# Writes of the down projections' operands issued from ACT's queue instead of SP's

## The chip, the cores and the metric

The kernel runs on one core of one Trainium2 chip. Its engines work side by side, each through its own list of instructions in order: PE (matrix products), DVE (vector work), ACT (activations, casts and copies), POOL and SP. SP computes nothing; here it issues the transfers (DMAs) between DRAM and the core's memory SBUF. An issue on any engine starts a transfer, which lands some microseconds later; instructions that need it wait on a semaphore. The metric is the device time of one execution in microseconds, given as the median of several runs.

## The reference, cut to what matters

A trunk of two layers on one sequence of 1024 positions with 1024 channels, all in float32. Layer 0 mixes positions by a Fourier transform and neighbourhood attention, layer 1 by a gated short convolution. Each layer then has a cross-attention to 256 memory tokens and a gated feed-forward block with a convolution over positions. The change touches the operands of the last product of the short-convolution mixer and of both feed-forward blocks:

```
def short_gated_conv_mixer(h, w_in, conv_w, w_out):
    z = h @ w_in
    gate_b, gate_c, u = ...            # three pieces of 1024 columns
    return (gate_b * dwconv3_centred(gate_c * u, conv_w)) @ w_out

def conv_ffn(h, w_up, conv_w, conv_b, w_down):
    z = h @ w_up                       # 1024 -> 4096
    u = z[..., :D_FF]                  # D_FF = 2048
    g = dwconv3_centred(z[..., D_FF:], conv_w) + conv_b
    return (jax.nn.gelu(g, approximate=False) * u) @ w_down
```

## The kernel before

**Arithmetic.** Every float32 operand is split in two parts that PE takes at its faster rate: ACT casts the high part (line 225) and DVE subtracts it from the value to get the low part (line 226). A product is then three matmuls: high by high (line 230), high by low (line 231), low by high (line 232).

**Seven products for eight.** The large products are done in Strassen's manner: the weight matrix and the data are cut in 2 x 2 blocks, and seven products of sums of blocks replace eight of blocks. The sums of weight blocks are made by POOL's transfers with accumulation into DRAM tensors named ws_u (up) and ws_d (down), and loaded by line 1083. The sums of the data's blocks are made on DVE.

**The feed-forward block.** For each block of 128 channels the up product runs its seven products; `up_post` makes gate, convolution (lines 1008 to 1011: ACT begins it, DVE adds the two neighbours) and gelu (line 1321), multiplies, and leaves two buffers of 128 x 1024. `put_rest` makes from them the sums that the down product needs: t1 (line 1240), t2 (1241), t3 (1243), t4 (1245). Each of the seven pieces, 128 x 512 or 256 KB, goes through `put`. `put` writes it to a DRAM tile xd_d (feed-forward) or xd_oc (mixer), 132 times in all; a few pieces of the last block stay in SBUF by a copy on ACT (`stays`). The down product reads the tiles back at line 1429, 512 KB at a time, and splits them again.

**Buffers.** SBUF has 52 places of 128 x 1024 and a few half ones, used over and over. A buffer that a write reads cannot be overwritten before that write has landed; the next user, often the cast of line 225, waits for it.

**Order.** The program is emitted by generators that run ahead of one another. Then the framework orders each engine's instructions by a simulated timeline of its own (line 1761: `tile.TileContext(nc, schedule_with_timeline_sim=True)`). So an edit in one place can shift the order on other engines too. In this kernel all of the transfers started by the hardware path are issued by SP, in SP's order: loads of weights (line 1083), writes of `put` (line 1226), reads back (line 1429), and spills and reloads of the residual. ACT issues none. Every transfer takes one of eight shared completion semaphores in turn, and an issue waits until the transfer that used the same one before has landed.

Of the kernel before, what the change touches and what calls it, by code (L numbers as in the profile page):

```python
# [43 lines left out]
U = 512  # L44
# [49 lines left out]
class Pool:  # L94
# [29 lines left out]
    def put(self, u, n=1):  # L124
        Pool.tick += 1
        for i in range(u, u + n):
            assert self.used[i]
            self.used[i] = False
            self.freed[i] = Pool.tick


class Kern:
# [1085 lines left out]
    def put(self, tag, s, k, p, src):  # L1218

        o = (k % 2) * U  # L1220
        if self.stays(tag, s, k // 2, p):
            if k % 2 == 0:
                self.xs[tag, p] = yield from self.alloc(F32)
            self.nc.scalar.copy(self.xs[tag, p].f(o, o + U), src)
        else:
            self.nc.sync.dma_start(self.xd_tile(tag, s, p, k // 2)[:, o:o + U], src)
        self.did.add((tag, "x", s, p, k))

    @staticmethod
# [536 lines left out]
```

## Time and profile before

| what | us |
|---|---|
| median of 3 runs | 2195.08 (2186.97 to 2198.77) |
| the profiled execution's own time | 2190.69 |
| its span in the profile | 2188.9 |
| PE busy | 2155.6 (98%) |
| DVE busy | 1461.0 (67%) |
| ACT busy | 966.0 (44%) |
| POOL busy | 342.1 (16%) |

The time of an engine at work is summed over its instructions; issuing transfers and waiting on semaphores is not counted as busy. PE is at work nearly all the time, so what matters is where it is not, and where its granted clock is below 1.00: there the same matmul takes longer and counts as busy. The feed-forward up products lie at about 740 to 1065 us (layer 0) and 1770 to 1990 us (layer 1), the mixer's down product of layer 1 at about 1360 to 1430 us.

### The profile page before, as it was taken

The page shows a single profiled execution, that of the slowest core. Times are in us where ns is not written, and L with a number is a line of the kernel's source. Part 1 is how long each engine was busy: PE and PEld are TensorE (multiplying, and loading weights), DVE is VectorE, ACT ScalarE, POOL GpSimd, SP SyncE. Part 2 cuts the span into 40 slices and gives each one's busy share as a digit, 9 for nine tenths or more (in the row PEclk, how much of TensorE's full clock was granted, in tenths as well). Part 3 has the DMA queues.
Part 4 walks back from the last instruction along what each step waited for, and adds up shares of the span by engine and source line. Part 5 has one row for each costly group of instructions (what it writes and reads, how often), then busy time and mean ns, then how long its engine had stood idle before and what let it go on. Part 6 is the DMA issues. An engine that isn't in the chain of part 4 may idle for free.

```text
span 2188.9 us, 27021 instructions
## 1 busy us (share of the span) xinstructions
PE 2155.6 (98%) x10174; PEld 1783.6 (81%) x10174; DVE 1461.0 (67%) x2001; ACT 966.0 (44%) x1506; POOL 342.1 (16%) x446
## 2 busy tenths in 40 slices
PE   9999999999999999999999999999999999999998
PEld 9988888888888777887888888778888878888887
DVE  6755456575667576667777667777566758757774
ACT  6532444354545333345445223535444534334643
POOL 5222122222211122111111100010111000000003
PEclk9999999999999999999999999999999999999999
DMA  9467677788877677899986567965656635447742
GB/s 376 151 158 186 157 183 221 189 207 234 216 202 221 180 191 219 245 277 355 270 267 151 162 193 204 342 162 150 177 163 184 183 101 182 150 135 258 242 154 77
DMA packets 176163, 441.92 MB, mean 202 GB/s; under 512 B 19616, under 2 KB 87456, under 8 KB 173856
## 3 DMA queue, kind: packets, MB, share of 16 engines
q1 hardware_dynamic: 99616, 305.95, 39.5%
q0 software_dynamic: 76416, 134.25, 29.9%
q8 instruction: 79, 1.29, 0.2%
q14 instruction: 52, 0.43, 0.1%
HBM read 384.54 MB, written 189.79 MB: 262 GB/s over the span
## 4 chain that ended last, share of the span: by engine, by line
PE 89%; DVE 5%; DMA 4%; ACT 1%; issue 1%; SPq 0%; DVEq 0%; ACTq 0%
PE PS L231 29%; PE PS L232 29%; PE PS L230 29%; DVE p L226 2%; PE PS L935 1%; DMA p<-in_w_out_dram 1%; ACT p L225 1%; DMA xd_d<-p 1%; DMA p<-in_w_down_dram 1%; DVE p L1009 1%; DMA p<-xd_d 1%; DVE p L1011 0%; DMA p<-ws_u 0%; DMA p<-xd_oc 0%; PE PS L333 0%
## 5 line engine op out<-in xcount | busy, mean ns | idle before, releaser
L230 PE MATMUL PS<-p,p 128*128 128x512 f32 (+1 forms) x3264 | 1222.7, 379 | 14.3 <-ACT p L225 13.4
L231 PE MATMUL PS<-p,p 128*128 128x512 f32 (+1 forms) x3264 | 1230.1, 378 | 5.1 <-DVE p L226 4.9
L232 PE MATMUL PS<-p,p 128*128 128x512 f32 (+1 forms) x3264 | 1218.5, 377 | 2.3 <-DVE p L226 2.3
L226 DVE TENSOR_TENSOR p<-p,p 128x1024 fp32r<-128x1024 f32 (+1 forms) x549 | 607.9, 1124 | 266.6 <-ACT p L225 219.1
L225 ACT CAST p<-p 128x1024 fp32r<-128x1024 f32 (+1 forms) x566 | 530.5, 959 | 542.3 <-PE PS L232 87.1
L230 PEld LDWEIGHTS PS<-p,p 128*128 128x128 f32 x3264 | 615.5, 189 | 140.0 <-ACT p L225 18.3
L231 PEld LDWEIGHTS PS<-p,p 128*128 128x128 f32 x3264 | 615.5, 189 | 125.7 <-DVE p L226 7.5
L232 PEld LDWEIGHTS PS<-p,p 128*128 128x128 f32 x3264 | 615.1, 189 | 121.4 <-DVE p L226 3.2
L317 ACT ACTIVATE p<-p 128x512 f32<-128x512 f32 (+1 forms) x128 | 74.4, 589 | 102.9 <-DVE p L816 39.9
L323 DVE TENSOR_TENSOR p<-p,p 128x512 f32<-128x512 f32 (+1 forms) x111 | 80.0, 723 | 31.5 <-ACT p L317 29.1
L226 DVE TENSOR_TENSOR p<-PS,p 128x512 fp32r<-128x512 f32 (+3 forms) x92 | 67.8, 744 | 41.4 <-ACT p L225 41.0
L1604 POOL TENSOR_TENSOR p<-p,p 128x512 f32<-128x512 f32 (+1 forms) x15 | 16.4, 1124 | 442.6 <-DVE p L497 425.0
L225 ACT CAST p<-PS 128x512 fp32r<-128x512 f32 (+3 forms) x92 | 57.5, 632 | 56.3 <-PE PS L232 31.4
L1075 POOL DMA_DIRECT2D ws_u<-gates x64 | 43.5, 778 | 205.0 <-ACT gates L1074 204.8
L816 DVE TENSOR_TENSOR p<-PS,p 128x512 f32<-128x512 f32 x64 | 43.5, 685 | 35.6 <-PE PS L232 35.5
L1008 ACT ACTIVATE p<-p,vec 128x1024 f32<-128x1024 f32 x32 | 39.7, 1241 | 61.1 <-DVE p L1317 48.4
L1009 DVE SCALAR_TENSOR_TENSOR p<-p,vec,p 128x1023 f32<-128x1023 f32 x40 | 51.2, 1279 | 21.7 <-ACT p L1008 21.1
L1076 POOL DMA_DIRECT2D ws_u<-in_w_up_dram x64 | 36.5, 591 | 175.2 <-DMA ws_u<-gates 175.1
L1077 POOL DMA_DIRECT2D ws_u<-ws_u x32 | 33.3, 1042 | 182.4 <-DMA ws_u<-in_w_up_dram 111.9
L1077 POOL DMA_DIRECT2D ws_u<-in_w_up_dram x32 | 33.6, 1050 | 140.1 <-DMA ws_u<-in_w_up_dram 113.1
L1321 ACT ACTIVATE p<-p 128x1024 f32<-128x1024 f32 x32 | 33.9, 1060 | 47.9 <-DVE p L1011 47.9
L1074 ACT COPY gates<-p 128x1 f32<-128x1 f32 x136 | 24.8, 191 | 68.4 <-DVE p L816 30.0
(171 smaller groups left out, 1300.8 us busy)
## 6 DMA issues: line engine op xcount, KB each, us to landing
ws_u<-in_w_up_dram POOLq DMA_DIRECT2D x96, 512.0 KB, 5.9
p<-ws_u SPq DMA_DIRECT2D x64, 512.0 KB, 4.4
xd_d<-p SPq DMA_DIRECT2D x104, 256.0 KB, 5.7
p<-xd_d SPq DMA_DIRECT2D x52, 512.0 KB, 6.3
ws_d<-in_w_down_dram POOLq DMA_DIRECT2D x48, 512.0 KB, 5.9
p<-in_w_up_dram SPq DMA_DIRECT2D x48, 512.0 KB, 4.8
ws_u<-ws_u POOLq DMA_DIRECT2D x32, 512.0 KB, 6.8
p<-in_wq_dram SPq DMA_DIRECT2D x32, 512.0 KB, 4.7
```

Of the source, the lines that this page charges most:

```text
L225: self.nc.scalar.copy(hi, src)
L226: (eng or self.nc.vector).tensor_tensor(lo, src, hi.bitcast(F32), op=ALU.subtract)
L230: mm(ps, whi, xhi, start=first, stop=False, skip_group_check=True)
L231: mm(ps, whi, xlo, start=False, stop=False, skip_group_check=True)
L232: mm(ps, wlo, xhi, start=False, stop=last, skip_group_check=True)
L317: nc.scalar.activation(t.f(0, w), src, AF.Square)
L323: nc.vector.tensor_tensor(st[ch].f(0, w), st[ch].f(0, w), t.f(0, w), op=ALU.add)
L816: self.nc.vector.tensor_tensor(hc, ps, hc, op=ALU.add)
L1008: nc.scalar.activation(tmp.f(), src, AF.Identity, scale=v[:, w[1]:w[1] + 1], bias=v[:, bias:bias + 1])
L1009: nc.vector.scalar_tensor_tensor(tmp.f(1, S), src[:, 0:S - 1], v[:, w[0]:w[0] + 1], tmp.f(1, S), op0=ALU.mult, op1=ALU.add)
L1075: g.dma_start(d[0:1, 0:1], gate[0:1])
L1077: g.dma_start(d, more, accum_op=ALU.add, max_dma_last_dim=1024)
```

## The change

`put` issues the same write on ACT in place of SP:

```
@@ -1223,7 +1223,7 @@
                 self.xs[tag, p] = yield from self.alloc(F32)
             self.nc.scalar.copy(self.xs[tag, p].f(o, o + U), src)
         else:
-            self.nc.sync.dma_start(self.xd_tile(tag, s, p, k // 2)[:, o:o + U], src)
+            self.nc.scalar.dma_start(self.xd_tile(tag, s, p, k // 2)[:, o:o + U], src)
         self.did.add((tag, "x", s, p, k))
```

In all 132 issues leave SP's list and stand in ACT's; no instruction is added. The framework's order of the other instructions shifts with it.

On ACT, at layer 0's first finished block of the up product (about 747 to 757 us): p_ is a buffer with its place's number, xd_d_0_6 is the down product's operand 6 of the first half.

```order
 L1321 ACTIVATE p_14_6510<-p_14_6510 128x1024
+L1226 DMA xd_d_0_5_0_6564<-p_19_6552 128x512
 L1074 COPY gates<-p_47_6108 128x1
+L1226 DMA xd_d_0_2_0_6516<-p_37_6031 128x512
+L1226 DMA xd_d_0_3_0_6566<-p_37_6031 128x512
 L1268 COPY p_14_6611<-p_48_6126 128x512
 L225 CAST p_33_6682<-p_25_6572 128x1024
+L1226 DMA xd_d_0_6_0_6556<-p_19_6552 128x512
+L1226 DMA xd_d_0_7_0_6559<-p_27_6553 128x512
+L1226 DMA xd_d_0_4_0_6562<-p_27_6553 128x512
 L1074 COPY gates<-p_43_6592 128x1
 L225 CAST p_37_6650<-p_6_6522 128x1024
```

Six of the block's writes now stand between ACT's gelu, copies and casts; three of them come behind the cast into p_33. The last row is the cast into p_37, the place that two of the writes read.

On SP, the same stretch: loads of weights and the writes that were between them.

```order
 L1083 DMA p_25_6572<-ws_u_1_3_1349 128x1024
 L1083 DMA p_10_6686<-in_w_up_dram 128x1024
-L1226 DMA xd_d_0_5_0_6564<-p_19_6552 128x512
-L1226 DMA xd_d_0_2_0_6516<-p_37_6031 128x512
-L1226 DMA xd_d_0_3_0_6566<-p_37_6031 128x512
-L1226 DMA xd_d_0_6_0_6556<-p_19_6552 128x512
-L1226 DMA xd_d_0_7_0_6559<-p_27_6553 128x512
 L1083 DMA p_1_6618<-ws_u_2_7_1350 128x1024
-L1226 DMA xd_d_0_4_0_6562<-p_27_6553 128x512
 L1083 DMA p_6_6732<-ws_u_2_3_1353 128x1024
```

Five writes stood in one run behind two loads, with the write of place p_19 (operand 6) fourth among them; now loads follow loads.

On DVE, in layer 0's up product at about 810 to 816 us: lines 1009 and 1011 are the convolution's two additions, line 226 the low part of an operand.

```order
 L1009 SCALAR_TENSOR_TENSOR p_17_6906<-p_44_6797,vec,p_17_6906 128x1023
+L1011 SCALAR_TENSOR_TENSOR p_17_6906<-p_44_6797,vec,p_17_6906 128x1023
 L1317 TENSOR_TENSOR p_50_6816<-PS,p_50_6816 128x512
+L226 TENSOR_TENSOR p_27_6992<-p_30_6859,p_19_6991 128x1024
+L226 TENSOR_TENSOR p_44_6986<-p_47_6823,p_14_6985 128x1024
 L1325 TENSOR_TENSOR p_7_6228<-PS,p_7_6228 128x512
-L1011 SCALAR_TENSOR_TENSOR p_17_6906<-p_44_6797,vec,p_17_6906 128x1023
-L226 TENSOR_TENSOR p_27_6992<-p_30_6859,p_19_6991 128x1024
+L1322 TENSOR_TENSOR p_7_6228<-p_7_6228,p_17_6906 128x512
 L1009 SCALAR_TENSOR_TENSOR p_10_6927<-p_50_6816,vec,p_10_6927 128x1023
 L1325 TENSOR_TENSOR p_45_6246<-PS,p_45_6246 128x512
-L226 TENSOR_TENSOR p_44_6986<-p_47_6823,p_14_6985 128x1024
```

The subtraction into p_44 moved up, ahead of two lines 1325 and the line 1009 of p_10.

On PE, at the first place: matmuls that take the operands p_37 and p_19.

```order
 L230 MATMUL PS<-p_11_6404,p_37_6650 128x512
 L231 MATMUL PS<-p_21_6405,p_37_6650 128x512
-L230 MATMUL PS<-p_11_6404,p_37_6650 128x512
-L231 MATMUL PS<-p_21_6405,p_37_6650 128x512
 L230 MATMUL PS<-p_3_6362,p_19_6614 128x512
 L231 MATMUL PS<-p_38_6363,p_19_6614 128x512
```

PE now comes to p_19 after two matmuls with p_37 instead of four.

## Rows read from the trace of the kernel before

**Rows 1.** The page: busy time of each engine; share of DMA queues; the chain's engines.

```profile
PE 2155.6 (98%) x10174; PEld 1783.6 (81%) x10174; DVE 1461.0 (67%) x2001; ACT 966.0 (44%) x1506; POOL 342.1 (16%) x446
...
q1 hardware_dynamic: 99616, 305.95, 39.5%
...
PE 89%; DVE 5%; DMA 4%; ACT 1%; issue 1%; SPq 0%; DVEq 0%; ACTq 0%
```

**Rows 2.** PE's waits, whole run: us in total, times, longest us.

```profile
PE PS L230 <- ACT p L225: 13.4, 9, 4.0
PE PS L231 <- DVE p L226: 4.9, 3, 2.6
```

**Rows 3.** Windows: length, busy us (x instructions) by engine, PEclk, DMA share, GB/s.

```profile
745.00:750.00 5.00, 5.00 (x23) 4.05 (x22) 4.96 (x8) 2.35 (x4) 0.51 (x1) 1.00 0.94 246
750.00:755.00 5.00, 4.43 (x19) 3.11 (x17) 4.31 (x7) 1.39 (x3) 0.09 (x1) 1.00 0.83 286
755.00:760.00 5.00, 1.59 (x4) 1.30 (x5) 1.39 (x2) 2.69 (x3) 1.33 (x2) 0.76 1.05 348
760.00:765.00 5.00, 5.00 (x15) 3.88 (x14) 2.45 (x2) 1.30 (x2) 0.50 (x1) 0.56 0.94 255
810.00:815.00 5.00, 3.44 (x15) 2.51 (x14) 5.00 (x7) 0.80 (x1) 0.57 (x2) 1.00 0.77 264
820.00:825.00 5.00, 3.15 (x15) 2.25 (x14) 2.80 (x4) 1.24 (x2) 0.31 (x1) 1.00 1.02 372
1420.00:1425.00 5.00, 3.54 (x15) 2.52 (x14) 5.00 (x7) 2.10 (x3) 0.00 (x0) 1.00 1.04 209
1425.00:1430.00 5.00, 3.87 (x10) 3.04 (x11) 5.00 (x6) 0.71 (x2) 0.00 (x0) 0.66 0.46 131
1785.00:1790.00 5.00, 3.26 (x13) 2.17 (x12) 3.15 (x5) 0.99 (x2) 0.00 (x0) 1.00 1.03 371
1790.00:1795.00 5.00, 4.64 (x14) 3.61 (x15) 3.58 (x3) 3.23 (x4) 0.00 (x0) 0.68 0.72 235
```

**Rows 4.** The chain of waits: start us, length us, what.

```profile
748.83 0.61 DVE p L1326
...
749.97 7.26 DMA xd_d<-p
757.31 1.05 ACT p L225
...
812.58 1.13 DVE p L226
...
816.18 5.98 DMA p<-ws_u
...
1783.62 5.54 DMA xd_d<-p
```

**Rows 5.** Line 1226's issues (ns min/median/max, first to last us), and their landings.

```profile
L1226 SPq DMA_DIRECT2D xd_d<-p x104: 319/376/1703, 744.6 to 2035.4; - x104
L1226 SPq DMA_DIRECT2D xd_oc<-p x28: 319/320/1342, 1235.6 to 1397.0; - x28
...
DMA to landing us min/median/max: 2.0/5.7/11.2
```

**Rows 6.** Timeline of SP: start us, us, line, operation, how many in a row.

```profile
748.60 0.33 SPq L1083 DMA_DIRECT2D p<-in_w_up_dram  x1
749.02 3.64 SPq L1226 DMA_DIRECT2D xd_d<-p  x5
```

**Rows 7.** DMA issues, 748.5 to 748.9 us, then whole run: KB each, us to landing.

```profile
p<-in_w_up_dram SPq DMA_DIRECT2D x1, 512.0 KB, 6.7
...
p<-ws_u SPq DMA_DIRECT2D x64, 512.0 KB, 4.4
```

**Rows 8.** Timeline of ACT: start us, us, instruction, [idle before it, for what].

```profile
747.04 1.06 ACT L1321 ACTIVATE p<-p 128x1024 f32<-128x1024 f32 x1 [1.12 <-DVE p L1011]
751.50 1.05 ACT L225 CAST p<-p 128x1024 fp32r<-128x1024 f32 x1 [1.36 <-DMA p<-ws_u]
...
970.88 1.05 ACT L225 CAST p<-p 128x1024 fp32r<-128x1024 f32 x1 [5.63 <-DMA xd_d<-p]
```

More of the change, by code (lines that the diff above doesn't have):

```diff
@@ L1225, in put @@
         else:
-            self.nc.sync.dma_start(self.xd_tile(tag, s, p, k // 2)[:, o:o + U], src)
+            self.nc.scalar.dma_start(self.xd_tile(tag, s, p, k // 2)[:, o:o + U], src)
         self.did.add((tag, "x", s, p, k))
```

## The prediction

> **What bounds the kernel now.** I read the page's busy shares first, then PE's waits over the whole run, then a table of 5 us windows, and last the chain of waits and the timelines of SP and ACT around the worst windows. The shares give the ceiling: PE is busy for 2155.6 us, 98% of the span, and the chain that ends last runs through PE for 89% of its length, through DVE for 5%, through DMA for 4% and through ACT for 1% [rows 1]. A queue that carries 39.5% of the DMA engines' time [rows 1] is not the bound of the whole; the change can only move the places where PE stands still or runs slowly.
>
> PE's waits are few. The reader is to see in them that the longest single one is 4.0 us and that the waits for ACT's casts (line 225, the high half of an operand) add to 13.4 us in nine waits, and those of one kind of matmul for DVE's subtraction (line 226, the low half) to 4.9 us in three [rows 2]. The windows turn this into a loss, idle time and slow clock together. A full window of 5 us has 23 matmuls at granted clock 1.00, so one is 5/23 = 0.217 us. Counting what is missing from 23 in each window [rows 3]:
> - A, layer 0's first finished block (750 to 765): 4 + 19 + 8 = 31 matmuls, 6.7 us. The clock falls to 0.76 and 0.56, the lower of the two levels (1.2 GHz for most of the last window), after PE had stood still.
> - F, the same place of layer 1 (1785 to 1795): 10 + 9 = 19, or 4.1 us, clock down to 0.68.
> - D, the mixer's down product (1420 to 1430): 8 + 13 = 21, or 4.6 us, clock down to 0.66.
> - B (810 to 815, 820 to 825): 8 + 8 = 16, or 3.5 us, clock 1.00 throughout.
>
> Together 87 matmuls, 18.9 us, under 1% of the time. No edit of a queue can win more than about that in these stretches.
>
> What ends the waits is read in the chain. At A, ACT's cast waits until a write xd_d, issued at 749.97, has landed 7.26 us later, because the cast overwrites the buffer that the write reads; the cast takes 1.05 us and PE goes on [rows 4]. At F it is the same kind of write, 5.54 us [rows 4]. At B the first gap waits for DVE's subtraction, and the second for a load p<-ws_u that takes 5.98 us [rows 4]. So the writes delay PE at A and F; at B something else does.
>
> **The change part by part.** It takes 132 issues (104 xd_d, 28 xd_oc) off SP and puts them on ACT; it adds no instruction.
>
> *Issue time.* At the median of the 104, 132 x 0.376 = 50 us [rows 5] of ACT's order are now issues. ACT is busy for 966.0 us of 2188.9 [rows 1], so this lies in its idle time: 0 us. If that cover is gone, as in front of a cast that PE waits for, four issues in a row (as at A) cost 4 x 0.32 = 1.3 us once; bounds 0 and +3 us.
>
> *Landing of the writes.* SP's timeline at A shows why the write took 7.26 us: a 512 KB load is issued at 748.60 and five writes follow from 749.02 on [rows 6]; the load itself lands after 6.7 us [rows 7], at 755.3, and the write of 749.97 at 757.2, behind it. The line's writes take 2.0 us at best, 5.7 in the median, 11.2 at worst [rows 5]. In one queue landings follow the issues; from two queues the engines can serve writes and loads side by side, so writes no longer wait for a load ahead of them. The bytes stay: 256 KB at the 348 GB/s of window 755 to 760 [rows 3] are 0.75 us, so what a write gains, a load beside it can lose.
>
> The Trainium skill ("DMA: Bandwidth & Descriptors", section "Issuing engines are not separate DMA queues") speaks against the change: DMAs started from several engines share the same 16 DMA engines, so spreading them saves only the sequencer's time to start them. By that the landings would not move, and the result would be the third rival's. The same page ("Queues, rings and completion order") says that a DMA engine takes turns between the rings that hold work, by which a write would be served next to the load; 749.97's landing behind the load agrees with one ring in order, and no trace so far shows two.
>
> *Place A.* ACT's new order decides it. The write of buffer p_37 stands ahead of the cast p_33, whose operand's load ends ACT's wait at 751.50 in the trace [rows 8]; the write of p_19 (d_6) stands behind that cast. The four writes ahead are 1 MB, 3 us alone and 6 us when shared in halves with loads. They can start at about 748, when the gelu ahead of them is done (747.04 + 1.06 [rows 8]), and the last at 749.5, when DVE has made its data (748.83 + 0.61 [rows 4]); so they land by 753 or 754 instead of 757.2. The cast p_37, behind three more issues, starts at about 754 and ends at 755.2, 3.2 us sooner than now (757.31 + 1.05 [rows 4]). What is late next is p_19: PE now takes only two matmuls of p_37 before it needs p_19, and its write is issued at about 753 and lands 2.0 to 5.7 us later, so its cast ends between 756.1 and 759.8. I take the middle, some 1.3 us of the 4.0 us idle saved and a quarter of the slow-clock cost (6.7 - 4.0 = 2.7): **-2.0 us**, bounds -6.7 (all gone) and +1.5 (p_19 at 759.8).
>
> *Place F* has the same chain with a shorter wait: half of A, **-1.0**; bounds -4.1 and +1.
>
> *Place B.* DVE's new order has the subtraction of p_44 ahead of three other instructions, so the first gap (1.7 us) should close. The second hangs on a load, which now shares with the writes on the other queue: 5.98 us plus one or two writes of 0.75, and its DVE predecessor comes some 0.4 us later. I take -1.7 + 2.2 = **+0.5**; bounds -3.5 (both close) and +5 (the second gap grows to A's 4.0 us and brings A's slow clock: 6.7 - 1.7).
>
> *Other loads.* There are 64 loads of B's kind, 4.4 us in the median [rows 7], and PE waits for few of them now: **+0.5**, bounds 0 and +4.1 (one more becomes a stall like F).
>
> *D* is DVE-bound, 5.00 busy of 5.00 in both windows [rows 3], and a queue does not speed DVE, though the new order moves a few instructions: **-0.5**, bounds -4.6 and +3 (half as much again). Between 960 and 1030 some writes now wait on ACT for an older DMA to finish, but ACT stands there anyway, 5.63 us until 970.88, for a write [rows 8]: nothing.
>
> Sum: 0 - 2.0 - 1.0 + 0.5 + 0.5 - 0.5 = **-2.5 us**. Against the profiled execution, 2190.69 us (span 2188.9), that is 2188.2; the median of the runs, 2195.08, lies 4.4 us higher, so I say **2192**.
>
> **The rivals.**
> *1. The writes were the whole trouble (faster).* If p_19's write lands early enough, A and F lose nothing, D keeps its clock, and B's first gap closes: -6.7 - 4.1 - 4.6 - 1.7 = -17, about 2178. For it: the chain names the write at A and F. Against it: d_6 behind a cast that waits for a load, DVE dense at D.
> *2. ACT blocks itself (slower).* An issue on ACT must wait for its data from DVE and for an older DMA; every cast behind it waits too, and PE takes these casts. On SP such a wait holds only later DMAs. One such stop that starves PE for 4 us costs what A does, 6.7 us; it decides from three new places on: 3 x 6.7 = 20, less A's and F's gain of 3, is +17, about 2212. For it: 132 new places for it, and landings of up to 11.2 us [rows 5]. Against it: ACT is 44% busy [rows 1], and PE has to wait for one kind of its casts only nine times now [rows 2], so most casts are made well ahead.
> *3. Nothing but the issuing changes (same).* Landings stay, A stays at 6.7 us, SP is freer without anyone waiting on SP: 2190 to 2196.
>
> **How the numbers follow.** Forecast 0.45, rival 3 0.15, rival 1 0.18, rival 2 0.22. A measurement of this kernel tells about 0.5%, 11 us, from no change: faster is under 2184, slower over 2206. The forecast and rival 3 lie within: 0.60 same; rival 1 gives 0.18 faster; rival 2 gives 0.22 slower. The bounds of the terms add to -18.9 and +17.6 us (3 + 1.5 + 1 + 5 + 4.1 + 3) and won't all fall on one side; the range goes to rival 1's time below and stops short of rival 2's above: 2178 to 2209.
>
> **What would show it.** A second hardware queue with 132 DMAs; landings of xd_d below 5.7 us and of p<-ws_u above 4.4 in the median. At A: cast p_37 before 757, then a wait for p_19's write, granted clock of 755 to 765 above 0.76 and 0.56. At F the same with 0.68. At B: no gap at 812, a longer one at 822. The forecast is wrong if landings stay, if PE waits for ACT more than 13.4 us in all, or if PE has waits at places where it has none now, with ACT standing at line 1226.

## The result, and the profile after

The changed kernel takes 2202.18 us (median of 14 runs, 2195.59 to 2214.06), the kernel before 2192.56 us (14 runs, 2183.96 to 2198.77) beside it. The ratio of the runs is 1.0052, with an interval of 1.0038 to 1.0067: 11.4 us slower by the ratio, 9.6 us by the two medians. The forecast was 2192 us, 2.5 us faster than before; the measured time lies in the stated range, but on the other side.

The profiled execution took 2208.06 us, 5.9 us above the median of its kernel; that of the kernel before, 2190.69 us, was 1.9 us below. So what one trace shows is read as places, not as a sum, and the other traces below show that even the places change from one execution to the next. The page of the changed kernel: busy times, queues and the chain's engines.

```profile
PE 2161.7 (98%) x10174; PEld 1786.2 (81%) x10174; DVE 1461.2 (66%) x2001; ACT 966.9 (44%) x1506; POOL 341.6 (15%) x446
...
q1 hardware_dynamic: 80608, 271.33, 34.9%
...
q10 hardware_dynamic: 19008, 34.61, 4.1%
...
PE 85%; DMA 7%; DVE 6%; ACT 1%; issue 1%; SPq 0%; ACTq 0%; DVEq 0%
```

A second hardware queue has appeared, with 34.61 MB, and the first has lost as much [rows 1]. Work did not grow: every engine is busy for within some microseconds of what it was. Only the chain moved, from PE to DMA and DVE. PE's waits in the whole run (us in total, times, longest):

```profile
PE PS L230 <- ACT p L225: 20.4, 13, 3.2
PE PS L231 <- DVE p L226: 4.8, 3, 2.5
PE PS L230 <- ACT p L1260: 2.2, 1, 2.2
...
PE PS L230 <- DVE p L1495: 1.4, 1, 1.4
```

The wait for casts rose from 13.4 to 20.4 us [rows 2]: more waits, none longer than the longest before. The line of the writes, now on ACT (ns min/median/max of an issue), and its landings; then the loads of weight sums:

```profile
L1226 ACTq DMA_DIRECT2D xd_d<-p x104: 326/327/2328, 746.0 to 2055.9; - x104
...
DMA to landing us min/median/max: 2.0/5.6/11.1
...
p<-ws_u SPq DMA_DIRECT2D x64, 512.0 KB, 4.7
```

A write lands after 5.6 us where it took 5.7 [rows 5], a load of sums after 4.7 where it took 4.4 [rows 7]. The second queue made the writes no faster.

The windows of the places (columns as in [rows 3], the engines in the order PE, PEld, which loads the weights, DVE, ACT, POOL; time runs 1 to 18 us later than before, as the lag grows). The first two rows are a stop ahead of all writes; A is 750 to 770, B is 810 to 830, 900 and 980 have no stop in the trace before, D is 1430 to 1445, F is 1795 to 1815:

```profile
560.00:565.00 5.00, 2.62 (x15) 1.94 (x14) 2.66 (x5) 3.16 (x6) 0.00 (x0) 1.00 0.79 128
565.00:570.00 5.00, 5.00 (x32) 4.52 (x33) 4.15 (x6) 3.31 (x10) 2.05 (x3) 1.00 0.55 75
...
750.00:755.00 5.00, 4.28 (x19) 3.23 (x18) 4.76 (x8) 1.67 (x2) 1.42 (x2) 1.00 0.83 317
755.00:760.00 5.00, 1.78 (x8) 1.14 (x8) 0.61 (x2) 1.24 (x2) 0.00 (x0) 1.00 1.08 319
760.00:765.00 5.00, 3.67 (x9) 2.37 (x9) 3.49 (x4) 2.94 (x3) 0.51 (x1) 0.50 0.60 205
765.00:770.00 5.00, 5.00 (x20) 4.00 (x19) 1.18 (x2) 0.00 (x0) 1.44 (x2) 0.81 0.69 159
810.00:815.00 5.00, 5.00 (x24) 4.11 (x23) 5.00 (x7) 2.46 (x3) 0.62 (x2) 1.00 0.31 73
820.00:825.00 5.00, 2.70 (x12) 1.87 (x10) 3.65 (x6) 1.51 (x2) 0.51 (x1) 0.99 1.03 326
825.00:830.00 5.00, 4.79 (x15) 3.83 (x16) 2.45 (x2) 2.09 (x3) 1.42 (x2) 0.67 0.83 269
900.00:905.00 5.00, 2.81 (x10) 1.91 (x9) 1.78 (x3) 2.13 (x4) 0.51 (x1) 0.84 0.87 155
905.00:910.00 5.00, 5.00 (x20) 3.99 (x19) 0.20 (x1) 0.59 (x1) 1.42 (x3) 0.82 0.64 221
980.00:985.00 5.00, 2.13 (x10) 1.41 (x9) 2.38 (x3) 2.37 (x4) 0.00 (x0) 1.00 1.10 334
985.00:990.00 5.00, 5.00 (x17) 3.93 (x16) 3.54 (x5) 2.64 (x6) 0.18 (x1) 0.66 1.09 359
1430.00:1435.00 5.00, 3.65 (x16) 2.70 (x15) 5.00 (x7) 5.00 (x7) 1.03 (x1) 1.00 0.78 226
1435.00:1440.00 5.00, 2.48 (x11) 1.59 (x10) 5.00 (x7) 2.20 (x3) 0.00 (x0) 0.93 0.76 112
1440.00:1445.00 5.00, 5.00 (x17) 3.98 (x17) 5.00 (x8) 1.05 (x1) 0.00 (x0) 0.73 0.65 210
1795.00:1800.00 5.00, 4.43 (x20) 3.28 (x19) 4.97 (x9) 1.83 (x3) 0.00 (x0) 1.00 0.94 299
1800.00:1805.00 5.00, 2.97 (x12) 1.69 (x10) 1.73 (x2) 1.09 (x2) 0.00 (x0) 0.95 0.85 330
1805.00:1810.00 5.00, 3.95 (x9) 3.14 (x10) 3.21 (x4) 2.90 (x3) 0.00 (x0) 0.50 0.50 150
1810.00:1815.00 5.00, 5.00 (x20) 4.00 (x19) 0.69 (x1) 0.00 (x0) 0.00 (x0) 0.87 0.16 63
```

Counted as in the prediction, 23 matmuls to a full window: A misses 4 + 15 + 14 + 3 = 36 where it missed 31; F 3 + 11 + 14 + 3 = 31 where it missed 19; D 7 + 12 + 6 = 25 where it missed 21; B's first gap is closed (24 in 810 to 815), its second misses 11 + 8 = 19, against 16 in its two windows before. The places at 900 and 980 miss 13 + 3 and 13 + 6, together 35, or 7.6 us. After each of these stops the granted clock is down in the next window. After the stop near 560, where PE waits 2.4 us for a cast behind a load, the clock stays at 1.00; it lies ahead of the first write (746.0), so the second queue did not make it, and when the writes begin this execution is already 1.3 us behind.

The chain of waits at these places (start us, length us, what): the two writes at A and F, the load at B, the write at 900, the load at 980.

```profile
753.16 7.93 DMA xd_d<-p
...
761.11 1.05 ACT p L225
...
818.14 5.95 DMA p<-ws_u
...
891.91 10.36 DMA xd_d<-p
...
968.92 13.76 DMA p<-in_w_down_dram
...
1798.24 6.63 DMA xd_d<-p
```

At A the write of p_19 is issued at 753.16, as foreseen, but takes 7.93 us. ACT's timeline there (as in [rows 8]) shows both casts late. Its first row is the gelu that stood at 747.04 before, so 1.3 us of every delay here are older than the writes:

```profile
748.35 1.06 ACT L1321 ACTIVATE p<-p 128x1024 f32<-128x1024 f32 x1 [1.12 <-DVE p L1011]
...
753.10 1.05 ACT L225 CAST p<-p 128x1024 fp32r<-128x1024 f32 x1 [0.32 <-DMA p<-ws_u]
753.16 1.85 ACTq L1226 DMA_DIRECT2D xd_d<-p  x3
755.10 0.19 ACT L1074 COPY gates<-p 128x1 f32<-128x1 f32 x1 [0.96 <-DVE p L1312]
758.72 1.04 ACT L225 CAST p<-p 128x1024 fp32r<-128x1024 f32 x1 [3.42 <-DMA xd_d<-p]
761.11 2.94 ACT L225 CAST p<-p 128x1024 fp32r<-128x1024 f32 x3 [1.34 <-DMA xd_d<-p]
```

The cast p_37 starts at 758.72 (757.31 before), p_19's at 761.11 (right behind p_37's before, at 758.4). Both wait for a write. Counted from the gelu, p_37's cast is late by 0.1 us and p_19's by 1.4 us. The forecast had p_37's at about 754.

At 980 the stop shows what two queues can do. Issues and landings (KB, us to landing) of the changed kernel in 968.9 to 969.1 and in 971.2 to 971.4:

```profile
p<-in_w_down_dram SPq DMA_DIRECT2D x1, 512.0 KB, 13.8
...
xd_d<-p ACTq DMA_DIRECT2D x1, 256.0 KB, 8.2
```

The load is issued at 968.9 and lands at 982.7; the write is issued 2.3 us later and lands at 979.4, ahead of it. In the kernel before the same load, issued at 961.9, and the same write behind it at 962.6 land in the order of issue, at 972.3 and 973.1:

```profile
p<-in_w_down_dram SPq DMA_DIRECT2D x1, 512.0 KB, 10.4
...
xd_d<-p SPq DMA_DIRECT2D x1, 256.0 KB, 10.5
```

So writes do pass loads now: followed through this trace, 15 of the 132 writes land ahead of a transfer that SP issued before them, while in the trace before none of SP's 682 transfers lands ahead of an earlier one. Here the load is what PE needs: its cast comes at 982.76, and PE stands until that is done.

### The profile page after: what moved, and what is told of

It is laid out like the page before. It is cut to its first block, busy times and chain, and to the rows that moved or that the text cites. A ratio compares the mean times of both kernels' runs of the same rounds, so it can differ in the third digit from the quotient of the medians.

```text
span 2206.3 us, 26961 instructions
## 1 busy us (share of the span) xinstructions
PE 2161.7 (98%) x10174; PEld 1786.2 (81%) x10174; DVE 1461.2 (66%) x2001; ACT 966.9 (44%) x1506; POOL 341.6 (15%) x446
## 3 DMA queue, kind: packets, MB, share of 16 engines
q10 hardware_dynamic: 19008, 34.61, 4.1%
## 4 chain that ended last, share of the span: by engine, by line
PE 85%; DMA 7%; DVE 6%; ACT 1%; issue 1%; SPq 0%; ACTq 0%; DVEq 0%
PE PS L231 28%; PE PS L232 27%; PE PS L230 27%; DVE p L226 2%; DMA xd_d<-p 1%; DMA p<-in_w_down_dram 1%; DMA p<-ws_u 1%; DMA xd_oc<-p 1%; DVE p L1009 1%; DMA p<-xd_oc 1%; DVE p L1011 1%; ACT p L225 1%; PE PS L935 1%; DMA p<-kvd 0%; DVE p L1325 0%
## 5 line engine op out<-in xcount | busy, mean ns | idle before, releaser
L230 PE MATMUL PS<-p,p 128*128 128x512 f32 (+1 forms) x3264 | 1225.2, 380 | 26.3 <-ACT p L225 20.4
L226 POOL TENSOR_TENSOR p<-p,p 128x1024 fp32r<-128x1024 f32 (+1 forms) x17 | 44.9, 2656 | 42.6 <-ACT p L225 42.2
```

Source lines behind the costliest of these rows:

```text
L226: (eng or self.nc.vector).tensor_tensor(lo, src, hi.bitcast(F32), op=ALU.subtract)
L230: mm(ps, whi, xhi, start=first, stop=False, skip_group_check=True)
```

## The experiments

All are timed against the kernel before on the same chip. Except for the changed kernel itself (after_again, s3_after), all pin the order: the instructions carry numbers in the order in which the program emits them, and those are the same before and after. After the program is emitted, each engine's instructions are tied into a given order by edges that fix the issue order and add no wait; in the programs and traces of these runs each engine's sequence is the one that it was tied to. (`pinned` gives the recorded order as lists of numbers; it is left out here.)

```
         k.all()
+        pin(tc)
...
+def pin(tc):
+    by = {i.name: i for i in tc.nc.cur_bb.bb.instructions}
+    info = mybir.DependencyInfo(mybir.DependencyClass.NoSync, mybir.DependencyReason.DATA)
+    for row in pinned():
+        row = [n for n in row if "I-%d" % n in by]
+        for a, b in zip(row, row[1:]):
+            tc.add_manual_dep(by["I-%d" % b], "I-%d" % a, info, reason="pinned order")
```

Old order and new order below mean those of the kernel before and of the changed kernel. So the edit's two effects, the queue and the order that the scheduler makes of it, can be had one at a time. The first theory was that ACT issues writes late. In the traces the mean time from the end of the DVE instruction that makes a write's data to the start of its issue, for the writes issued in 740 to 960 us (layer 0's up product), is 0.77 us before and 1.42 us after. The expectations below use a coarser count of the same thing, 0.6 and 1.3.

**order_only.** New order, queue as before:

```
-            self.nc.scalar.dma_start(self.xd_tile(tag, s, p, k // 2)[:, o:o + U], src)
+            self.nc.sync.dma_start(self.xd_tile(tag, s, p, k // 2)[:, o:o + U], src)
```

> The writes stay on SP; every other instruction of every engine is pinned to the order that it has in the changed kernel. Theory L (the loss comes from writes that ACT issues late, because they stand in its list behind instructions that wait): no late issue here, so the ratio to the kernel before is 0.997 to 1.003. Rival O (the shifted order of casts, subtractions and matmuls is what costs): 1.003 to 1.007, with PE's stalls near 756 and 981 us as in the changed kernel. Rival R (a second queue makes transfers land later): 0.997 to 1.003, as for L.

Measured: 1.0001 (0.9985 to 1.0017). The new order by itself costs nothing that can be told. The stops are there all the same: PE's waits of this kernel,

```profile
PE PS L230 <- ACT p L225: 15.2, 10, 3.0
PE PS L231 <- DVE p L226: 4.2, 3, 2.6
PE PS L230 <- ACT p L1260: 3.1, 1, 3.1
```

lie between those of before and after, though the time is that of the kernel before. The third is at 973 to 976 us, near the place where the changed kernel stops for a load: a stop there needs no second queue. At B the load that ends the second gap takes as long as in both of the others:

```profile
814.74 5.93 DMA p<-ws_u
820.69 1.05 ACT p L225
```

**queue_only.** The change's line, old order.

> The writes are on ACT; every other instruction is pinned to the order of the kernel before, and the scheduler alone places the writes in ACT's list. Theory L: 1.003 to 1.006, with the mean from data ready to issue in 740 to 960 us near the 1.3 us of the changed kernel (0.6 before). Rival O: 0.997 to 1.002. Rival R: 1.003 to 1.006, with issues as early as before but landings longer than 6.2 us in that stretch.

Measured: 1.0008 (0.9994 to 1.0023). The queue alone costs nothing that can be told either. Theory L asked for 1.003 or more, rival R as well. The writes were late here too, 1.02 us behind their data in the same stretch, if not as late as in the changed kernel.

**queue_early.** The same, with the writes' places in ACT's list pinned too.

> As queue_only, but each write is placed in ACT's list at the place where ACT stood, in the trace of the kernel before, when the write's data became ready. Theory L: most of the loss goes, 0.997 to 1.002, ready to issue below 0.9 us in 740 to 960 us. Rival R: the loss stays, 1.003 to 1.006, since there are still two queues. Rival O: 0.997 to 1.002. If two queues gave the writes any advantage, it would show here: landings below 5.6 us and a ratio under 0.997.

Measured: 1.0011 (0.9995 to 1.0027), issue 0.38 us after the data in 740 to 960 us. The landings of its 132 writes:

```profile
DMA to landing us min/median/max: 2.0/5.6/11.0
```

Issued with hardly any delay on a queue of their own, the writes land no sooner, and the kernel gains nothing. This is the clearest word on the forecast's gain: none shows. PE's waits at A are 3.9 us in this trace and 5.9 in the one of s3_queue_early (4.0 before), at F 3.3 and 4.3 (2.1 before).

**queue_layer0.**

```
-            self.nc.scalar.dma_start(self.xd_tile(tag, s, p, k // 2)[:, o:o + U], src)
+            (self.nc.scalar if tag == "d0" else self.nc.sync).dma_start(self.xd_tile(tag, s, p, k // 2)[:, o:o + U], src)
```

> As queue_only, but only the 52 writes of layer 0's feed-forward block are on ACT, the other 80 on SP. Theory L: writes got later by 0.7 us in the mean in layer 0's up product and hardly elsewhere, so most of the loss is here: 1.002 to 1.005. Rival O: 0.997 to 1.002. Rival R: layer 0's share by number of writes, about 0.4 of queue_only's loss: 1.001 to 1.003.

Measured: 1.0004 (0.9991 to 1.0017): with nothing lost by queue_only there was nothing to place.

None of the four showed the loss. So the changed kernel was timed again, together with kernels between it and its parts.

**after_again.** The changed kernel, word for word.

> The changed kernel itself, timed beside the next three. With the order alone and the queue alone each at a ratio of 1.000 to 1.001, the loss of 1.0052 is either of both together or of that one session. Theory I (both together: late writes cost only where the new order needs their buffers sooner): 1.004 to 1.006. Rival C (chance of a session): 0.999 to 1.002.

Measured: 1.0053 (1.0036 to 1.0070). Not chance.

**after_early.** New order, the writes earlier in ACT's list.

> The changed kernel with all its orders pinned, except that each write stands in ACT's list at the place where ACT was, in the trace of the changed kernel, when its data became ready. Theory I, by lateness: 0.998 to 1.002, with ready to issue below 0.6 us in 740 to 960 us (1.26 in the changed kernel). If the second queue as such costs with this order: 1.004 to 1.006. Rival C: as after_again.

Measured: 1.0034 (1.0021 to 1.0047), issue 0.42 us after the data. Most of the loss stays, though the writes are hardly late any more. Lateness may be a third of it; the intervals overlap, so even that isn't shown. As the account of the whole loss the first theory falls. The run says a second thing: this kernel is pinned and still loses, so pinning does not by itself hide the loss. At A in this kernel the write is issued at 751.99 and the chain is

```profile
751.99 8.28 DMA xd_d<-p
760.29 1.05 ACT p L225
```

so of what was won in issuing p_19's write (753.16 to 751.99), 0.35 us were lost in landing (7.93 to 8.28).

**act_order** and **pe_dve_order.** The new order on one half of the engines, the old on the other, queue changed.

> ACT (with its writes), SP and POOL pinned to the changed kernel's order, PE and DVE to the order of the kernel before. If the loss sits in the order of ACT's list and of SP's loads: 1.004 to 1.006. If it needs the new order of matmuls and subtractions: 0.999 to 1.002.

> The reverse: PE and DVE pinned to the changed kernel's order; ACT's other instructions, SP and POOL to that of the kernel before, with the writes on ACT where the scheduler puts them. If the loss needs the new order of matmuls and subtractions: 1.004 to 1.006; if it sits in ACT's and SP's order: 0.999 to 1.002.

Measured: 1.0050 (1.0032 to 1.0068) and 1.0053 (1.0034 to 1.0073). With the writes on ACT either half of the new order is as dear as the whole. That does not say that either half brings the queue's loss: a mixed order may cost by itself, and act_order was not timed with the writes on SP (for pe_dve_order see sp_pe_dve).

**s3_after, s3_queue_only, s3_order_only, s3_queue_early.** The first set had been timed without the changed kernel; here they stand together.

> The changed kernel once more, beside three kernels of the first set, which had been timed without it. If the sessions are alike: 1.004 to 1.006.

> queue_only again. If its 1.0008 holds beside the changed kernel, half of the new order (either half: ratios 1.0050 and 1.0053) turns the queue's effect from nothing into the whole loss: 1.000 to 1.002. If the first session differed from the others, the queue alone costs the loss: 1.004 to 1.006.

> order_only again. Orders alone cost nothing in any session: 0.998 to 1.002. If the first session hid the loss of the order too: 1.003 to 1.006.

> queue_early again. If lateness of the issues is the loss: below queue_only by at least 0.002 where queue_only is at 1.004 to 1.006. If the second queue itself is the loss: as queue_only.

Measured: 1.0049 (1.0033 to 1.0065), 1.0009 (0.9997 to 1.0022), 1.0006 (0.9991 to 1.0021), 1.0002 (0.9990 to 1.0014). Everything repeats. Queue alone and order alone add to 0.0015; together they are 0.005. This is the result that the document rests on.

**sp_pe_dve, q_pe, q_dve, q_act.** The first keeps the writes on SP; the others have the change's line and one engine's new order.

> Control for the mixed orders: PE and DVE pinned to the changed kernel's order, all else to that of the kernel before, writes on SP. If the half-changed order costs by itself: 1.003 to 1.006, and pe_dve_order's 1.0053 says nothing on the queue. If it costs only with the writes on ACT: 0.999 to 1.002.

> Writes on ACT; PE alone pinned to the changed kernel's order (it asks for operand p_19 after two matmuls in place of four), all else to the order of the kernel before. If PE's order is what makes the late buffers cost: 1.003 to 1.006; if not: 1.000 to 1.002, as queue_only.

> Writes on ACT; DVE alone pinned to the changed kernel's order, all else to that of the kernel before. If DVE's order (subtractions and sums of the writes' data moved against each other) is what costs with the queue: 1.003 to 1.006; if not: 1.000 to 1.002.

> Writes on ACT; ACT alone pinned to the changed kernel's order with its places for the writes, all else to the order of the kernel before. If the places of writes and casts in ACT's list are what costs: 1.003 to 1.006; if not: 1.000 to 1.002, and in act_order it was SP's order of loads.

Measured: 1.0027 (1.0007 to 1.0047), 1.0034 (1.0016 to 1.0051), 1.0072 (1.0053 to 1.0092), 1.0045 (1.0028 to 1.0062). A mixed order costs something with the old queue too: sp_pe_dve lies between the two ranges that were set for it, and its interval overlaps that of pe_dve_order (1.0034 to 1.0073), so how much of pe_dve_order's 1.0053 is the queue's is open. With the writes on ACT each engine's new order alone costs, DVE's most. But q_pe, q_dve and q_act have no twin with the writes on SP, so the cost can be the mixture's as well as the queue's. Since one engine's order costs more (1.0072) than all of them (1.0053), the parts don't add up to the whole. With the writes on ACT, the old order is the only one of those tried that came out free.

**a_d0** and **a_rest.** New order on all engines, the writes split by layer, as in queue_layer0 and the other way round (`tag != "d0"`).

> All engines pinned to the changed kernel's order; only layer 0's 52 feed-forward writes are on ACT, at the changed kernel's places, the other 80 on SP. By stages, three profiles of the changed kernel stand against two of order_only at +6 us in layer 0's feed-forward block and +5 us after it. If the loss is the sum of places: 1.001 to 1.004 here, and the same for a_rest. If it sits where the first stalls are, in layer 0: 1.004 to 1.006.

> The complement: all engines pinned to the changed kernel's order; the 28 writes of the mixer and layer 1's 52 on ACT, layer 0's on SP. Sum of places: 1.001 to 1.004, and the two together near 1.005. All in layer 0: 0.999 to 1.002.

Measured: 1.0020 (1.0007 to 1.0032) and 1.0023 (1.0011 to 1.0035), together 0.0043 of the 0.005. By place the loss does add up: about half from the 52 writes of layer 0, half from the 80 later ones. So it is not the stops at 900 and 980 alone.

**The places in other traces.** PE's waits, summed, in us, in 745 to 775 (A), 805 to 840 (B), 885 to 960, 960 to 1010 and 1775 to 1820 (F), one trace each:

| trace | A | B | 900 | 980 | F |
|---|---|---|---|---|---|
| before | 4.0 | 3.4 | 0.0 | 0.0 | 2.1 |
| order_only, s3_order_only | 4.1, 5.7 | 2.5, 2.0 | 0.0, 0.0 | 3.1, 1.2 | 3.5, 3.2 |
| queue_only, s3_queue_only | 5.7, 5.4 | 5.0, 3.6 | 0.0, 4.4 | 2.3, 0.4 | 2.8, 3.0 |
| the changed kernel, three times | 5.2, 5.0, 4.4 | 2.5, 6.0, 1.9 | 2.2, 0.0, 2.0 | 2.9, 4.9, 1.1 | 3.7, 4.2, 3.6 |

Except by a little at F, no place sets the changed kernel apart from its two halves. A stop at 980 comes with one queue too, and F's wait grows by the order alone. The two profiled executions of queue_only are also the longest of its 12 each time (2203.60 and 2205.79 us). So the traces show what a stop is made of, and the timed runs alone show what the change costs.

No version beat the kernel before.

## Why the prediction was wrong

The direction was wrong: 2.5 us faster was forecast, about 11 us slower came. The prediction's own signs of being wrong appeared: landings stayed, and PE waited 20.4 us for casts, more than 13.4. Step by step:

- **Ceiling and places.** Right as a reading: PE's stops are where things changed. What the forecast left out is that a kernel at 98% with few stops has far more room to get new ones.
- **Issue time on ACT, 0.** Not contradicted: an issue takes 0.327 us in the median, ACT's busy time is unchanged, and with the old order the queue costs under 0.0023 in all.
- **Landing of the writes.** This step failed, and with it the sign. "Writes no longer wait for a load ahead of them" is true of the order of landing (the pass at 980), not of the time: 5.7 to 5.6 us, and 5.6 in queue_early. In 750 to 760 the DMA share is 0.83 and 1.05 before, 0.83 and 1.08 after; a write that passes a load there still shares the engines with it, as the forecast itself said of the load. The Trainium skill's sentence on issuing engines ("DMA: Bandwidth & Descriptors", "Issuing engines are not separate DMA queues") had it right for the landings. The third rival, which went by it, had the landings right and the time, 2190 to 2196, wrong.
- **A, -2.0.** The last write of p_37, which the forecast had landed by 753 or 754 so that the cast could come 3.2 us sooner, was issued at 751.7 (forecast 749.5) and took 6.9 us, and 8.7 and 8.1 us in the two other traces of the changed kernel, where it took 7.26 before; the cast was no sooner. (The forecast put four writes in front of the cast p_33; ACT's list has three there.) The issue of p_19's write at 753 was foreseen; its landing, bounded at 5.7 us by the median of the run, was 7.93. In the two other traces it was 5.3 and 5.7, so that bound failed in one trace of three; the landing of p_37's write failed in all. In this execution 36 matmuls are missing in place of 31, +1.1 us. **F, -1.0**: 31 in place of 19, +2.6 us. F rested on the same landing; its wait also grew with the writes on SP (3.5 us in order_only, 2.1 before), so its loss is not the second queue's alone.
- **B, +0.5.** Near in size, +0.7 us (19 in place of 16, the clock at 0.67 behind the second gap), by another way than forecast. The first gap closed, as foreseen. But the load of the second took 5.95 us where it took 5.98, so it did not become longer by sharing; with the writes on SP and the new order (order_only) it takes 5.93 and PE waits as long, 2.5 us. What this trace shows at B is the order. In the two other traces of the changed kernel the load took 8.7 and 5.4 us.
- **D, -0.5**: no gain. 25 matmuls are missing in place of 21, +0.9 us. PE's wait for the low part, 2.5 us, is what it was (2.6 [rows 2]); a wait for another DVE line (1495) rose from 0.6 to 1.4 us.
- **960 to 1030, "nothing"**, and **other loads, +0.5, at most one more stop**. These were too small for this execution: stops at 900 and 980, 7.6 us. The forecast looked only at whether ACT's wait covered the writes' wait, and not at the load that shares with them. The median of the 64 loads of sums rose from 4.4 to 4.7 us as foreseen, but it is 4.8 in order_only, so this is no sign of the second queue.
- **Shifted order.** Priced at two or three places and taken as nothing elsewhere. By itself that holds (1.0001, 1.0006). With the queue it fails: the same order then costs 0.004 more than with the old queue. The prediction had no term for the two together, and this is where the measured loss lies.
- **Rival 2** gave the direction. Its mechanism, ACT blocking itself, is at most a part: after_early keeps 0.0034. It asked for three new stops of 6.7 us; two smaller ones came, and older ones grew.

Shown by runs: neither the queue nor the order costs by itself what can be told, both together cost 0.005, and with the new order the cost of the queue is spread over both layers. Read from single traces only: what each stop waits for, at A, F and 900 a write, at 980 a load that writes have passed. Open: why the old order bears two queues and the new one does not. No single engine's order explains it, and two profiles of the changed kernel lie 11.3 us apart (spans 2209.2 and 2197.9 us), as much as the loss itself.

## What to carry to other kernels

Moving a transfer to another engine's queue is two edits where a scheduler sets the order: pin the order, time each alone and both together before explaining either, and time a mixed order on the old queue too. Where the DMA engines are as busy as here (a share of 0.8 to 1.1), a second queue may change who lands first and not how long it takes; look which of the passed transfers the bound engine waits for. Bound a landing by what its own place showed, not by the median of the run. And before a stop in one trace is called new, look for it in a second trace of the same kernel.

## What the runs showed of the hardware

Transfers of two queues were served side by side: a 256 KB write issued on ACT 2.3 us after a 512 KB load on SP landed 3.3 us ahead of it, where in one queue they landed in order, 0.8 us apart. Within a queue the landings followed the issues throughout (682 on SP before; 550 on SP and 132 on ACT after); across the two, 15 writes landed ahead of an earlier transfer of SP.

The time to landing of the 132 writes hardly changed with the queue and the delay of the issue: in the median 5.7 us on SP (5.9 with the new order), 5.6 on ACT, 5.6 on ACT with early issue.

Stops of PE of about the same length did not all end alike: one of 2.2 us (900) fell in a window with a granted clock of 0.84 and was followed by 0.82, one of 2.5 us (B) by 0.67, one of 2.9 us (980) by 0.66, two at A, 4.5 us together, by 0.50 and 0.81; one of 2.4 us (560) was followed by 1.00.
